# Opening of a two-layer encoder: where the squares are summed, where fillers stand, and where a quarter's rows are multiplied

## The chip, the cores and the metric

The kernel runs on one core of a Trainium2 chip. The metric is the device time of one execution, in microseconds (us), lower is better. The core's engines run side by side, each through its own list of instructions in a fixed order, and wait for each other through semaphores: TensorE (PE: matmuls; PEld is its loading of weights), VectorE (DVE), ScalarE (ACT), GpSimd (POOL) and SyncE (SP, which here issues the loads).

## What is computed

A trunk of two layers is applied to a sample of 512 tokens and a prompt of 256 tokens, each of width 1024, all in float32. Layer 0 mixes with an mLSTM in both directions, layer 1 with windowed attention; behind each comes a feed-forward network with a short convolution. Each of the four blocks begins with a normalization that is shifted and scaled by rows computed from a condition vector `c`:

```python
for l in range(DEPTH):
    mod = jax.nn.silu(c) @ adaln_w[l] + adaln_b[l]
    sh1, sc1, g1, sh2, sc2, g2 = [t[:, None, :] for t in jnp.split(mod, 6, axis=-1)]
    h = rmsnorm(x, norm_g[l, 0]) * (1 + sc1) + sh1
    proj = h @ w_in  # the mixer begins
    ...
    x = x + g1 * y
    h = rmsnorm(x, norm_g[l, 1]) * (1 + sc2) + sh2
    x = x + g2 * conv_ffn(h, ...)
return rmsnorm(x, final_g)
```

What matters here is the very first step of layer 0: `sh1` and `sc1` (2048 columns of `silu(c) @ adaln_w[0]`), the first normalization, and the first products `h @ w_in`.

## The kernel before

`x` lies transposed: 128 partitions, 8 chunks `c` of the width, 768 columns (columns 0 to 255 are the prompt, 256 to 767 the sample). The sample is normalized in two ranges of 256 columns, `r0` and `r1`; the prompt is `r2`. Products in float32 that must be precise are made of three: a high part and a low part of each operand (`hi`, `lo` for weights, `hh`/`hl`, with the tiles `zh`/`zl`, for the normalized input), and high x high, low x high, high x low are added in PSUM.

The method `opening` does everything up to the first four weight tiles' products (`i` = 0 is the gates' narrow weight, 1 and 2 the first query halves, 3 the first key half). In the part this is about, the order of PE, ACT, DVE and SP is the order in which the code is written (`manual_schedule`). Its steps:

- SP loads, in this order: the sample of `x` (4 loads), quarter 0's rows (4 loads), the narrow weight, the first weight's two halves, the rows of quarters 1 to 3 (12 loads; the last four go to `raw` buffers, of which there are five, and wait there for the narrow weight and the weight halves to be split), the prompt of `x`, and more.
- Statistics of the sample: `squares` (ACT, L919) squares each chunk into a buffer `nt`; `total` (PE, L927) multiplies the squares by a 128x2 tile of 1/1024 (`inv`), chunk by chunk into one PSUM group; `power` (DVE L935, POOL L936) adds EPS and raises to -1/2; `spread` (PE, `pa<-kct,nr`) spreads the result over the partitions into `pr`.
- Rows, for one quarter `i` of the 1024 columns (chunks 2i and 2i+1): `modulation(i, js)` (PE, L948) multiplies four blocks `j` of the loaded rows by the condition; `out` (DVE L957, ACT L958) copies the sums from PSUM; `turn` (PE, L962) turns them to the partitions; `factors` (DVE L969 to L971) makes shift and gain; `scaled` (DVE L974, ACT L975) makes `zh` of a chunk; `lower` (DVE L978) makes `zl`.
- `cast` and `rest` (ACT and DVE, L889 and L890) split a weight half.
- `sample(i, c)` is the three products of weight tile `i` and chunk `c` for the 512 sample columns (128x512, `ps<-zh,whi` and the like); `prompt(i, c)` is the same for the prompt.
- `warm(spare, n)` is `n` products of a tile of ones into a PSUM bank that is overwritten later: fillers.
- The prompt's statistics go through the class `Norm`: squares on ACT (L113), added on POOL (L122), and `next(factor)` brings first the total and the power (PE `pa<-inv,nt`, DVE L162, POOL L163) and then the spread.

In the profile, all products that go through the helper `mm` have the line L270. A 128x128 or 128x2 product in float32 leaves two records, a 32x256 product of `modulation` two as well.

Of the kernel before, what the change touches and what calls it, by code (L numbers as in the profile page):

```python
# [14 lines left out]
ALU = mybir.AluOpType  # L15

P = 128
D = 1024
KC = D // P
# [163 lines left out]
class Net:  # L183
# [660 lines left out]
    def opening(self, pool, sinks):  # L844

        nc, io = self.nc, self.io
# [3 lines left out]
        r0, r1, r2 = RANGES  # L850
# [49 lines left out]
        def sample(i, c, *za):  # L900
            for z, a in za or ((0, 0), (1, 0), (0, 1)):
                mm(z, i, a, c, S0, S1, 0, c == KC - 1 and (z, a) == (0, 1))
# [10 lines left out]
        turned = self.pa()  # L913
        half = {}

        def squares(rng, cs):
            for c in cs:
                sq = self.tmp([P, 256])
                act(sq, x(c)[:, rng[0] : rng[1]], AF.Square)  # L919
                half[rng, c] = sq  # L920

        def total(rng, cs):
            for c in cs:
                if c == 0:
                    half[rng] = self.pa()
                for b in range(2):
                    nc.tensor.matmul(  # L927
                        half[rng][:, 2 * b : 2 * b + 2], half[rng, c][:, b * P : (b + 1) * P], self.inv,
                        start=c == b == 0, stop=c == KC - 1, skip_group_check=True,
                    )  # L930

        def power(rng):
            r = half[rng, "r"] = self.nt.tile([P, 2], F32, tag="nr", name=self.nm("nr"), bufs=3)
            mean = half[rng][:, :4].rearrange("p (b s) -> p b s", s=2)[:, :, 0]
            nc.vector.tensor_scalar(r, mean, EPS, None, ALU.add)  # L935
            nc.gpsimd.tensor_tensor(r, r, self.mhalf[:, :2], ALU.pow)  # L936
# [6 lines left out]
        def modulation(i, js):  # L943
            for j in js:
                for z in range(2):
                    for g in range(2):
                        r = 32 * (2 * z + g)
                        nc.tensor.matmul(  # L948
                            sums[r : r + 32, :256], self.silc[:, 2 * j + z, :], rows[4 * i + j][:, z, 256 * g : 256 * g + 256],
                            start=j == 0, stop=j == 3, skip_group_check=True,  # L950
                        )
# [3 lines left out]
        def out(i):  # L955
            sides[i] = [self.tmp([P, P]) for _ in range(2)]
            nc.vector.tensor_copy(sides[i][0], sums[:, :P])  # L957
            nc.scalar.copy(sides[i][1], sums[:, P : 2 * P])  # L958
# [5 lines left out]
        def factors(i):  # L964
            c = 2 * i
            got = turned[:, 8 * i : 8 * i + 8].rearrange("p (b g s) -> p b g s", b=2, g=2)
            wide = lambda at: self.cst(at, 2).unsqueeze(2).to_broadcast([P, 2, 2])
            mod = self.mod[0]
            tt(mod[:, 8 + c : 10 + c], got[:, :, 1], wide(AB + 8 + c), ALU.add)  # L969
            stt(self.gain[0][0][:, c : c + 2], mod[:, 8 + c : 10 + c], 1.0, wide(NG + c), ALU.add, ALU.mult)  # L970
            tt(mod[:, c : c + 2], got[:, :, 0], wide(AB + c), ALU.add)  # L971

        def scaled(c):
            stt(x(c)[:, S0:S1], x(c)[:, S0:S1], gain(c, 0), pr, ALU.mult, ALU.mult)  # L974
            act(self.hh[:, c, S0:S1], x(c)[:, S0:S1], AF.Identity, bias=shift(c, 0))  # L975
# [18 lines left out]
        with self.tc.manual_schedule(engines={eng.PE, eng.Activation, eng.DVE}):  # L994
            for i in range(4):
                bank[i, 0] = self.ps()
            spare = bank[3, 0]
            squares(r0, range(KC))
            total(r0, range(KC))
            power(r0)  # L1000
            squares(r1, range(KC))
            modulation(0, (0,))
            spread(r0)
            total(r1, range(4))
            modulation(0, (1,))
            total(r1, range(4, KC))
            power(r1)
            modulation(0, (2,))
            spread(r1)
            self.warm(spare, 4)  # L1010
            modulation(0, (3,))
            out(0)
            self.warm(spare, 4)
            turn(0)
            narrow3 = narrow.rearrange("p (j m) -> p j m", m=4)
            hi0, lo0 = (t.rearrange("p (j m) -> p j m", m=32)[:, :, 0:4] for t in (hi[0], lo[0]))
            nc.scalar.copy(hi0, narrow3)
            tt(lo0, narrow3, hi0.bitcast(F32), ALU.subtract)
            factors(0)
            cast(1)  # L1020
            scaled(0)
            scaled(1)
            lower(0)
            rest(1)
            lower(1)
            cast(2)
            rest(2)
            self.warm(spare, 14)

            sample(0, 0)  # L1030
            sample(0, 1)
            modulation(1, (0,))
            for i in (1, 2):
                for c in (0, 1):
                    sample(i, c, *ph)
                if i == 1:
                    modulation(1, (1,))
            for i in (1, 2):
                for c in (0, 1):
                    sample(i, c, *pl)  # L1040
            modulation(1, (2,))
            self.warm(spare, 4)
            modulation(1, (3,))
            out(1)
            self.warm(spare, 4)
            turn(1)
            factors(1)
            for c in (2, 3):
                scaled(c)
            for c in (2, 3):  # L1050
                lower(c)
            modulation(2, (0,))
            self.warm(spare, 8)
            modulation(2, (1,))
            for i in range(3):
                sample(i, 2)
            modulation(2, (2,))
            sample(0, 3)
            modulation(2, (3,))
            out(2)  # L1060
            sample(1, 3)
            sample(2, 3)
            turn(2)
            factors(2)
            for c in (4, 5):
                scaled(c)
            for c in (4, 5):
                lower(c)
            modulation(3, (0,))
            modulation(3, (1,))  # L1070
            for i in range(3):
                sample(i, 4)
            modulation(3, (2,))
            sample(0, 5)
            modulation(3, (3,))
            out(3)
            sample(1, 5)
            sample(2, 5)
            turn(3)
            factors(3)  # L1080
            for c in range(4):
                norm.square(c)
            for c in (6, 7):
                scaled(c)
            for c in (6, 7):
                lower(c)
            for c in range(4, KC):
                norm.square(c)
            for z, (t0, t1) in enumerate(((0, 640), (640, 1024))):
                a, b = (kw[y][z].rearrange("p k m -> p (k m)") for y in range(2))  # L1090
                self.fp_copy_split(a, b, keys[:, t0:t1])
            self.warm(spare, 8)
            for c in (6, 7):
                for i in range(3):
                    sample(i, c)
            next(factor)
            for c in range(4):
                sample(3, c)
            next(factor, None)
            for c in range(4, KC):  # L1100
                sample(3, c)
            c0, c1, q = r2
            for i in range(3):
                bank[i, 1] = self.pa()

            def first(c):
                t = self.tmp([P, c1 - c0])
                stt(t, x(c)[:, c0:c1], gain(c, q), got[r2], ALU.mult, ALU.mult)
                act(self.hh[:, c, c0:c1], t, AF.Identity, bias=shift(c, q))
                return t  # L1110

            ts = {0: first(0)}
            for c in range(KC):
                if c + 1 < KC:
                    ts[c + 1] = first(c + 1)
                if c == 1:
                    sinks[0](0, bank[0, 0])
                if c in (3, 5):
                    sinks[c // 2](0, bank[c // 2, 0])
                stt(  # L1120
                    self.hl[:, c, c0:c1], ts.pop(c), shift(c, q), self.hh[:, c, c0:c1].bitcast(F32), ALU.add, ALU.subtract
                )
                for i in range(3):
                    prompt(i, c)
            bank[3, 1] = self.ps()
            for c in range(KC):
                prompt(3, c)
            self.opened = self.ahead(U_MIN + 1, 1)
            sinks[3](0, bank[3, 0])
# [828 lines left out]
```

## Time and profile before

| | |
|---|---|
| median of 3 runs | 1816.17 us (1815.19 to 1816.62) |
| the profiled execution | 1814.75 us, span 1813.0 us |
| mean granted TensorE clock | 0.998 |
| PE busy | 1779.3 us (98% of the span) |
| DVE busy | 1379.6 us (76%) |
| ACT busy | 895.3 us (49%) |
| POOL busy | 508.6 us (28%) |
| HBM | 176.77 MB read, 101 GB/s over the span |

All times inside the profile count from the span's start. A busy PE is not a PE at its peak, since matmuls are pipelined; the chain of waits tells more than the shares. In the first 45 us the loads are dense: the page's first slice moves 325 GB/s, against 102 GB/s on the average.

### The profile page before, as it was taken

The numbers are of one execution on the slowest core, as the hardware profiler recorded it, in microseconds if no ns is written. First come the engines' busy times: TensorE is split into PE (matmuls) and PEld (weight loads), VectorE is DVE, ScalarE is ACT, GpSimd is POOL, SyncE is SP. The second block draws the span as 40 slices with busy tenths as digits, with TensorE's granted clock in tenths as the row PEclk, the third lists the DMA queues.
The fourth block names the chain that finished last, engine by engine and source line by source line (L and its number), as shares of the span: only waits on it lengthen the run. The fifth ranks groups of instructions, "written<-read, shape, count | busy, mean of one in ns | idle before, by whom it ended". The sixth has DMA issues, their size and how long they took to land.

```text
span 1813.0 us, 28950 instructions
## 1 busy us (share of the span) xinstructions
PE 1779.3 (98%) x11220; PEld 1653.8 (91%) x11220; DVE 1379.6 (76%) x2183; ACT 895.3 (49%) x1810; POOL 508.6 (28%) x424
## 2 busy tenths in 40 slices
PE   8999999999999999999999999999999999999998
PEld 6798888989998999999999999889989999999998
DVE  2597777995799777777777867767998777777777
ACT  3445534454465444444444556665564444444443
POOL 0201210231024333333331313330144333333323
PEclk9999999999999999999999999999999999999999
DMA  8254556556212222222222321134122222222212
GB/s 325 71 176 157 199 190 213 186 179 206 81 57 78 63 70 70 66 64 69 70 70 83 117 88 47 54 96 131 56 82 70 70 70 70 70 70 70 70 36 70
DMA packets 64597, 185.09 MB, mean 102 GB/s; under 512 B 6231, under 2 KB 24311, under 8 KB 64332
## 3 DMA queue, kind: packets, MB, share of 16 engines
q1 hardware_dynamic: 63884, 182.72, 31.3%
q8 instruction: 88, 1.44, 0.3%
q10 hardware_dynamic: 576, 0.52, 0.1%
q14 instruction: 49, 0.40, 0.1%
HBM read 176.77 MB, written 6.44 MB: 101 GB/s over the span
## 4 chain that ended last, share of the span: by engine, by line
PE 83%; DVE 7%; DMA 4%; ACT 3%; issue 2%; POOL 1%; SPq 0%; POOLq 0%; DVEq 0%; ACTq 0%
PE ps L270 25%; PE pa L270 23%; PE ps L1447 10%; PE ps L1448 10%; PE ps L1450 10%; DMA raw<-in_adaln_t_dram 2%; DVE junk L480 2%; DMA raw<-in_w_dram 2%; PE pa L1286 1%; PE pa L927 1%; DVE wlo L277 1%; ACT whi L276 1%; PE pa L948 1%; PE pa L1447 0%; PE pa L1448 0%
## 5 line engine op out<-in xcount | busy, mean ns | idle before, releaser
L276 ACT CAST whi<-raw 128x1024 fp32r<-128x1024 f32 x229 | 239.7, 1048 | 341.1 <-PE pa L270 144.2
L277 DVE TENSOR_TENSOR wlo<-raw,whi 128x1024 fp32r<-128x1024 f32 x229 | 312.1, 1364 | 121.6 <-ACT whi L276 119.2
L270 PE MATMUL pa<-slab,whi 128*128 128x256 f32 (+1 forms) x1280 | 307.9, 336 | 0.0
L270 PEld LDWEIGHTS pa<-slab,whi 128*128 128x128 f32 x1280 | 222.1, 188 | 21.8 <-DVE slab L539 0.4
L539 DVE SCALAR_TENSOR_TENSOR slab<-pa,mod,slab 128x256 f32<-128x256 f32 (+1 forms) x320 | 187.2, 603 | 60.8 <-PE pa L270 60.7
L270 PE MATMUL pa<-slab,wlo 128*128 128x512 f32 (+1 forms) x640 | 205.5, 334 | 0.0
L270 PE MATMUL ps<-zh,whi 128*128 128x256 f32 (+1 forms) x520 | 178.9, 344 | 1.1 <-ACT zh L975 1.0
L1447 PE MATMUL ps<-zh,whi 128*128 128x384 f32 x504 | 172.4, 342 | 3.9 <-ACT nt L1518 2.0
L270 PE MATMUL ps<-zl,whi 128*128 128x256 f32 (+1 forms) x520 | 174.1, 336 | 0.8 <-DVE zl L505 0.5
L270 PE MATMUL ps<-slab,whi 128*128 128x384 f32 (+2 forms) x704 | 172.4, 330 | 2.2 <-ACT sg L838 1.3
L270 PE MATMUL ps<-zh,wlo 128*128 128x256 f32 (+1 forms) x520 | 173.0, 335 | 0.3 <-DVE wlo L277 0.3
L1448 PE MATMUL ps<-zl,whi 128*128 128x384 f32 x504 | 169.8, 337 | 0.8 <-DVE zl L1404 0.8
L1450 PE MATMUL ps<-zh,wlo 128*128 128x384 f32 x504 | 168.9, 335 | 0.0
L480 DVE CUSTOM_DVE_ANT_0 junk<-raw,crow,cstt 128x1024 f32<-128x1024 f32 x112 | 148.3, 1324 | 25.7 <-DMA raw<-in_adaln_t_dram 24.9
L1483 POOL TENSOR_TENSOR raw<-raw,raw 128x512 f32<-128x512 f32 x40 | 54.0, 1349 | 317.6 <-DVE wlo L277 245.5
L270 PEld LDWEIGHTS pa<-slab,wlo 128*128 128x128 f32 x640 | 120.5, 188 | 13.4 <-DVE wlo L277 0.4
L1699 POOL TENSOR_TENSOR slab<-slab 128x772 f32<-128x772 f32 x44 | 86.4, 1965 | 164.2 <-DVE slab L1687 152.2
L270 PEld LDWEIGHTS ps<-slab,whi 128*128 128x128 f32 x704 | 122.4, 188 | 4.9 <-ACT sg L838 1.5
L1686 DVE SCALAR_TENSOR_TENSOR slab<-slab,cstt,slab 128x771 f32<-128x771 f32 x88 | 103.8, 1181 | 26.6 <-ACT slab L1684 26.4
L270 PE MATMUL ps<-slab,wlo 128*128 128x384 f32 (+2 forms) x352 | 114.7, 327 | 0.1
L270 PEld LDWEIGHTS ps<-zh,whi 128*128 128x128 f32 x520 | 98.4, 189 | 17.3 <-issue 6.0
L1687 DVE SCALAR_TENSOR_TENSOR slab<-slab,cstt,slab 128x771 f32<-128x771 f32 x88 | 110.2, 1252 | 0.8
(316 smaller groups left out, 4320.9 us busy)
## 6 DMA issues: line engine op xcount, KB each, us to landing
raw<-in_w_dram SPq DMA_DIRECT2D x208, 512.0 KB, 3.8
raw<-in_adaln_t_dram SPq DMA_DIRECT2D x56, 512.0 KB, 4.5
raw<-in_adaln_w_dram SPq DMA_DIRECT2D x24, 512.0 KB, 4.6
slab<-in_x_dram SPq DMA_DIRECT2D x12, 512.0 KB, 6.0
slab<-in_adaln_h_dram SPq DMA_DIRECT2D x12, 512.0 KB, 9.2
slab<-mrows SPq DMA_DIRECT2D x8, 384.0 KB, 5.1
xs<-slab SPq DMA_DIRECT2D x6, 512.0 KB, 3.6
bt<-brow SPq DMA_DIRECT2D x16, 192.0 KB, 3.1
```

The source lines that it names most:

```text
L270: self.nc.tensor.matmul(out, lhsT, rhs, start=start, stop=stop)
L276: nc.scalar.copy(hi, src)
L277: return nc.vector.tensor_tensor(lo, src, hi.bitcast(F32), ALU.subtract)
L480: nc.vector.tensor_tensor_reduce(out=junk, in0=w, in1=row[:, s], scale=1.0, scalar=self.cst(AB + 48 * l + j), op0=ALU.mult, op1=ALU.add, a ...
L539: return self.nc.vector.scalar_tensor_tensor(x, o, self.mod[l][:, gc + c, q : q + 1], x, ALU.mult, ALU.add)
L1447: mm(o, wh[:, k], hi[k], start=start and k == 0, stop=False, skip_group_check=True)
L1448: mm(o, wh[:, k], lo[k], start=False, stop=False, skip_group_check=True)
L1450: mm(o, wl[:, k], hi[k], start=False, stop=k == 3, skip_group_check=True)
L1483: tt(q[0], q[2], q[0], ALU.subtract)
L1686: stt(y[:, 1:], u[:, :-1], w(0), y[:, 1:], ALU.mult, ALU.add)
L1687: stt(y[:, :-1], u[:, 1:], w(2), y[:, :-1], ALU.mult, ALU.add)
L1699: nc.gpsimd.tensor_tensor(y, y, yrow[:, j], ALU.mult)
```

## The change

Within `opening`, five things:

- The squares of a range are added up on DVE, seven adds of 128x256 for each range, into the first square's buffer, and `total` is one product for each half of the range instead of eight.
- Fillers: 30 ahead of range 0's total, 3, 2 and 2 between the next pieces, 3 and 10 (before: 4 and 14) ahead of the first products; those in quarters 1 to 3 shrink from 4, 4, 8 and 8 to one pair.
- `lower` of chunk 1 and `cast(2)` stand ahead of the first `rest`.
- The blocks, copies and turn of quarter i+1 stand among the products of quarter i (a helper `tiles` with a table of what follows which product), so that a turn comes two products (of three matmuls each) before the end of the quarter in front.
- The total of the prompt's squares comes after three of the eight last-tile products (before: ahead of all), the spread after six (before: after four).

The lists of ACT, POOL and SP are the same in both kernels, and behind the opening those of PE and DVE too. PE's list at its start, before (`inv` is the tile of 1/1024, `nt` are squares, `slab` with `silc` are rows and condition, `kct` with `nr` the spread):

```order
L927 MATMUL pa_193<-inv,nt_189 128x2 x2
L927 MATMUL pa_193<-inv,nt_191 128x2 x2
L948 MATMUL pa_169<-slab_111,silc 32x256 x4
L270 MATMUL pa_168<-kct,nr_210 128x128 x2
L927 MATMUL pa_235<-inv,nt_213 128x2 x2
L927 MATMUL pa_235<-inv,nt_215 128x2 x2
L927 MATMUL pa_235<-inv,nt_217 128x2 x2
L927 MATMUL pa_235<-inv,nt_219 128x2 x2
L948 MATMUL pa_169<-slab_111,silc 32x256 x4
```

and now, from PE's first instruction (`ones` are fillers):

```order
L270 MATMUL ps_176<-ones 128x128 x30
L270 MATMUL pa_230<-inv,nt_177 128x2 x2
L270 MATMUL ps_176<-ones 128x128 x3
L947 MATMUL pa_169<-slab_111,silc 32x256 x4
L270 MATMUL pa_168<-kct,nr_233 128x128 x2
L270 MATMUL ps_176<-ones 128x128 x2
L947 MATMUL pa_169<-slab_111,silc 32x256 x4
L270 MATMUL pa_274<-inv,nt_236 128x2 x2
L270 MATMUL ps_176<-ones 128x128 x2
L947 MATMUL pa_169<-slab_111,silc 32x256 x4
L270 MATMUL pa_168<-kct,nr_277 128x128 x2
L947 MATMUL pa_169<-slab_112,silc 32x256 x4
```

Of 32 two-column products four are left, and the fillers stand in front and between. DVE's list at the same place had nothing between its four memsets and the two adds of EPS; now:

```order
L921 TENSOR_TENSOR nt_177<-nt_177,nt_194 128x256
L921 TENSOR_TENSOR nt_177<-nt_177,nt_197 128x256
L934 TENSOR_SCALAR nr_233<-pa_230 128x2
L921 TENSOR_TENSOR nt_236<-nt_236,nt_238 128x256
L921 TENSOR_TENSOR nt_236<-nt_236,nt_241 128x256
```

The add of EPS of range 0 (L934), which reads range 0's total from PE, stands ahead of all adds of range 1. PE's list between quarter 1 and quarter 2, before (the L962 pair is turn 1, the products behind are chunk 2's):

```order
L270 MATMUL ps_175<-zh,wlo_161 128x512 x2
L948 MATMUL pa_169<-slab_113,silc 32x256 x4
L270 MATMUL ps_176<-ones 128x128 x4
L948 MATMUL pa_169<-slab_113,silc 32x256 x4
L270 MATMUL ps_176<-ones 128x128 x4
L962 MATMUL pa_170<-cstt,nt_350 128x4
L962 MATMUL pa_170<-cstt,nt_351 128x4
L948 MATMUL pa_169<-slab_113,silc 32x256 x4
L270 MATMUL ps_176<-ones 128x128 x8
L948 MATMUL pa_169<-slab_114,silc 32x256 x4
L270 MATMUL ps_173<-zh,whi_156 128x512
```

and now:

```order
L270 MATMUL ps_175<-zh,wlo_161 128x512 x2
L961 MATMUL pa_170<-cstt,nt_356 128x4
L961 MATMUL pa_170<-cstt,nt_357 128x4
L947 MATMUL pa_169<-slab_113,silc 32x256 x4
L270 MATMUL ps_176<-ones 128x128 x2
L947 MATMUL pa_169<-slab_114,silc 32x256 x4
L270 MATMUL ps_173<-zh,whi_156 128x512
L270 MATMUL ps_173<-zh,wlo_159 128x512
L270 MATMUL ps_173<-zl,whi_156 128x512
L947 MATMUL pa_169<-slab_114,silc 32x256 x4
```

Two of quarter 1's blocks have moved up in front of these rows, the turn follows the products at once, and quarter 2's third block stands behind the first three products of quarter 1.

```diff
-        def squares(rng, cs):
-            for c in cs:
+        def squares(rng):
+            for c in range(KC):
                 sq = self.tmp([P, 256])
                 act(sq, x(c)[:, rng[0] : rng[1]], AF.Square)
-                half[rng, c] = sq
...
+                if c:
+                    tt(half[rng], half[rng], sq, ALU.add)
+                else:
+                    half[rng] = sq
+
+        def total(rng):
+            pm = self.pa()
+            for b in range(2):
+                self.mm(pm[:, 2 * b : 2 * b + 2], half[rng][:, b * P : (b + 1) * P], self.inv, True, True)
+            half[rng] = pm
...
+            squares(r0)
+            self.warm(spare, 30)
+            total(r0)
             power(r0)
-            squares(r1, range(KC))
+            squares(r1)
+            self.warm(spare, 3)
             modulation(0, (0,))
             spread(r0)
-            total(r1, range(4))
+            self.warm(spare, 2)
             modulation(0, (1,))
-            total(r1, range(4, KC))
+            total(r1)
             power(r1)
+            self.warm(spare, 2)
             modulation(0, (2,))
             spread(r1)
-            self.warm(spare, 4)
             modulation(0, (3,))
...
+            def tiles(k, between):
+                for n, (c, i) in enumerate((c, i) for c in (2 * k, 2 * k + 1) for i in range(3)):
+                    sample(i, c)
+                    for f, *a in between.get(n, ()):
+                        f(*a)
+
+            operands(1)
+            tiles(1, {
+                0: [(modulation, 2, (2,))],
...
+            operands(2)
+            tiles(2, {0: [(modulation, 3, (2,))], 1: [(modulation, 3, (3,)), (out, 3)], 3: [(turn, 3)]})
             factors(3)
...
-            self.warm(spare, 8)
-            for c in (6, 7):
-                for i in range(3):
-                    sample(i, c)
-            next(factor)
-            for c in range(4):
+            tiles(3, {})
+            for c in range(KC):
                 sample(3, c)
-            next(factor, None)
-            for c in range(4, KC):
-                sample(3, c)
+                if c in (2, 5):
+                    next(factor, None)
```

More of the change, by code (lines that the diff above doesn't have):

```diff
@@ L914, in opening @@
         half = {}
-        def squares(rng, cs):
-            for c in cs:
+        def squares(rng):
+            for c in range(KC):
                 sq = self.tmp([P, 256])
                 act(sq, x(c)[:, rng[0] : rng[1]], AF.Square)
-                half[rng, c] = sq
[L922 to L930, printed above, removed]
+                if c:
[7 more added lines that the diff above has]
+            half[rng] = pm
         def power(rng):
@@ L997, in opening @@
             spare = bank[3, 0]
-            squares(r0, range(KC))
-            total(r0, range(KC))
+            squares(r0)
+            self.warm(spare, 30)
+            total(r0)
             power(r0)
-            squares(r1, range(KC))
+            squares(r1)
+            self.warm(spare, 3)
             modulation(0, (0,))
             spread(r0)
-            total(r1, range(4))
+            self.warm(spare, 2)
             modulation(0, (1,))
-            total(r1, range(4, KC))
+            total(r1)
             power(r1)
+            self.warm(spare, 2)
             modulation(0, (2,))
             spread(r1)
-            self.warm(spare, 4)
             modulation(0, (3,))
             out(0)
-            self.warm(spare, 4)
+            self.warm(spare, 3)
             turn(0)
@@ L1023, in opening @@
             lower(0)
-            rest(1)
             lower(1)
             cast(2)
+            rest(1)
             rest(2)
-            self.warm(spare, 14)
+            self.warm(spare, 10)
             sample(0, 0)
+            modulation(1, (0,))
             sample(0, 1)
-            modulation(1, (0,))
+            modulation(1, (1,))
             for i in (1, 2):
@@ L1035, in opening @@
                     sample(i, c, *ph)
-                if i == 1:
-                    modulation(1, (1,))
+                modulation(1, (i + 1,))
+            out(1)
             for i in (1, 2):
@@ L1040, in opening, with operands @@
                     sample(i, c, *pl)
[L1041 to L1045, printed above, removed]
-            turn(1)
[L1047 to L1051, printed above, removed]
+            turn(1)
             modulation(2, (0,))
-            self.warm(spare, 8)
+            self.warm(spare, 2)
             modulation(2, (1,))
-            for i in range(3):
[L1056 to L1079, printed above, removed]
+            def operands(i):
+                factors(i)
+                for c in (2 * i, 2 * i + 1):
+                    scaled(c)
+                for c in (2 * i, 2 * i + 1):
+                    lower(c)
+            def tiles(k, between):
[6 more added lines that the diff above has]
+                0: [(modulation, 2, (2,))],
+                1: [(modulation, 2, (3,)), (out, 2)],
+                3: [(turn, 2), (modulation, 3, (0,))],
+                5: [(modulation, 3, (1,))],
+            })
+            operands(2)
+            tiles(2, {0: [(modulation, 3, (2,))], 1: [(modulation, 3, (3,)), (out, 3)], 3: [(turn, 3)]})
             factors(3)
@@ L1091, in opening @@
                 self.fp_copy_split(a, b, keys[:, t0:t1])
-            self.warm(spare, 8)
-            for c in (6, 7):
-                for i in range(3):
-                    sample(i, c)
-            next(factor)
-            for c in range(4):
+            tiles(3, {})
+            for c in range(KC):
                 sample(3, c)
-            next(factor, None)
-            for c in range(4, KC):
-                sample(3, c)
+                if c in (2, 5):
+                    next(factor, None)
             c0, c1, q = r2
```

## The prediction

> **What bounds the kernel now.** In the page's chain of work that ended last TensorE (PE) stands first by far, so a saving must be a wait or work of PE that vanishes. I then read that chain in order of time over the first 120 us, since all edits lie in the first 85 us (columns: start, length, what), and the groups of the first 75 us (count, then busy us and mean ns of one):
>
> ```profile
> 6.32 0.42 ACT nt L919
> 6.79 6.99 PE pa L927 x32
> 13.77 1.01 PE pa L948 x8
> ...
> 24.77 1.22 PE pa L270 x4
> ```
>
> ```profile
> L927 PE MATMUL pa<-inv,nt 128*128 128x2 f32 x64 | 14.0, 351 | 6.8 <-ACT nt L919 6.8
> L270 PE MATMUL ps<-zh,wlo 128*128 128x512 f32 x24 | 8.9, 392 | 0.0
> ```
>
> The opening is bound by PE itself until 28.7: from 6.79 it is never idle, and the sums of squares (L927, 64 records of two columns) hold it for 14 us. All of it runs at half speed. The timeline (start, length, engine, line) shows that speed, and the marks against which I measure:
>
> ```profile
> 0.83 0.17 DVE L377 MEMSET ones<- 128x128 f32 x1 [0.83 <-PEq L1938]
> 6.32 2.61 ACT L919 ACTIVATE nt<-slab 128x256 f32<-128x256 f32 x8 [1.83 <-DMA slab<-in_x_dram]
> 25.79 1.91 PE L270 MATMUL ps<-ones 128*128 128x128 f32 x8
> 28.69 0.29 DVE L957 COPY nt<-pa 128x128 f32<-128x128 f32 x1 [4.75 <-PE pa L948]
> 29.83 3.37 PE L270 MATMUL ps<-ones 128*128 128x128 f32 x28
> 31.18 1.38 ACT L975 ACTIVATE zh<-slab,mod 128x512 fp32r<-128x512 f32 x2 [0.70 <-DVE slab L974]
> 32.96 0.48 PE L270 MATMUL ps<-zh,whi 128*128 128x512 f32 x1
> 62.95 0.50 PE L270 MATMUL ps<-zh,whi 128*128 128x512 f32 x1
> ```
>
> A filler is two records. Eight took 1.91 us at 25.8 (about 0.21 each from start to start), and 28 took 3.13 us between 29.83 and 32.96 (0.112 each). The full rate came about 3.7 us after dense products began at 24.77. The granted clock of the profile's rows reads full throughout and does not show it.
>
> Three marks, then: quarter 0's rows copied out at 28.69, first sample product S at 32.96, last quarter's first product T at 62.95.
>
> **Term A, start to the first copy-out.** The data limit this once PE does not. Landings, by windows that hold single issues (issue time, then time to landing):
>
> ```profile
> 9.91 1.81 ACT L919 ACTIVATE nt<-slab 128x256 f32<-128x256 f32 x5 [0.98 <-DMA slab<-in_x_dram]
> 4.89 0.43 SPq L406 DMA_DIRECT2D slab<-in_x_dram  x1
> DMA to landing us min/median/max: 6.3/6.3/6.3
> L862 SPq DMA_DIRECT2D slab<-in_adaln_h_dram x2: 430/576/722, 6.5 to 7.3; - x2
> DMA to landing us min/median/max: 8.5/8.8/9.1
> ```
>
> The second 256 columns of x land at 9.9 and 11.2, quarter 0's last rows at 7.3 + 9.1 = 16.4. SP's order and its waits up to there are unchanged, so these times stand.
>
> The added DVE work: 14 adds of 128x256. No such row exists in f32; the nearest are the 128x384 add and a 128x4 add, with the pow that follows:
>
> ```profile
> L122 DVE TENSOR_TENSOR nt<-nt,nt x26: 549/552/559, 440.4 to 1279.4; 128x384 f32<-128x384 f32 x26
> L969 DVE TENSOR_TENSOR mod<-pa,cstt 128x4 f32<-128x4 f32 x4 | 0.7, 163 | 4.4 <-PE pa L962 4.3
> 14.05 0.70 POOL L936 TENSOR_TENSOR nr<-nr,mhalf 128x2 f32<-128x2 f32 x1 [11.48 <-DVE nr L935]
> ```
>
> By size between 0.16 and 0.55 it is 0.42, with 0.04 for each add's wait on the one before: 0.46, so seven take 3.2 us. The first can start at about 7.1 (6.32, one square every 0.31, 0.42 long): range 0's sum stands at 10.3. The 30 fillers (60 records) start at 1.0: with the rate rising after 3.7 us, 17 records take 3.7 and 43 take 4.8, end 9.5; never rising, 60 x 0.213 = 12.8, end 13.8. I take 9.5 to 11, since the rise has no fixed time. So the fillers lie beside the load and the adds, and cost nothing unless the rate stays low.
>
> Range 0's total on PE (four records, 0.6 with its end) stands at 11.0. Behind it, on DVE, the small add of EPS (0.16) stands in front of range 1's seven adds: a new wait, behind which all range 1 is queued. These run 11.1 to 14.3; ScalarE's last square waits for the same total (it reuses that buffer) but is done by 12.6. Total 14.9, EPS add and pow to 15.9, spread (0.5) 16.4, then the modulation's last block. From that block's start to the copy is 0.71 (40.93 to 41.64 below): 17.1. With late fillers 17.8; I take **17.4, so A = 11.3** (at half speed throughout about 22, A = 6.6; at best the rows' landing sets 17.1, 11.6).
>
> **Term B, copy-out to S.** Before 4.27. The 28 filler records after the turn become 20: 0.9 off, and then zh (31.18 + 0.73, that is 3.2 after the copy) arrives at the same time. **B = 0.9** (0 to 1; at half speed -2).
>
> **Term C, S to T.** The rows of one quarter's end before, and the PE rates:
>
> ```profile
> 40.93 0.64 PE L948 MATMUL pa<-slab,silc 128*32 128x256 f32 x8
> 41.64 0.29 DVE L957 COPY nt<-pa 128x128 f32<-128x128 f32 x1 [6.02 <-PE pa L948]
> 42.50 0.51 PE L962 MATMUL pa<-cstt,nt 128*128 128x4 f32 x4
> 42.93 0.64 PE L948 MATMUL pa<-slab,silc 128*32 128x256 f32 x8
> 44.22 1.38 ACT L975 ACTIVATE zh<-slab,mod 128x512 fp32r<-128x512 f32 x2 [1.93 <-DVE slab L974]
> 47.78 0.39 PE L270 MATMUL ps<-zh,wlo 128*128 128x512 f32 x1
> 48.00 0.39 PE L270 MATMUL ps<-zl,whi 128*128 128x512 f32 x1
> 48.32 0.64 PE L948 MATMUL pa<-slab,silc 128*32 128x256 f32 x8
> 48.89 0.50 PE L270 MATMUL ps<-zh,whi 128*128 128x512 f32 x1
> 54.34 0.50 PE L270 MATMUL ps<-zh,whi 128*128 128x512 f32 x1 [0.99 <-ACT zh L975]
> ```
>
> A product costs 0.23. A modulation block adds 0.66 (48.00 to 48.89 is 0.89, less 0.23), a turn 0.43. From turn to the first zh is 2.4 us (42.50 to 44.22 + 0.7). Before: 54 x 0.23 + 12 x 0.66 + 3 x 0.43 + 48 filler records x 0.112 = 12.4 + 7.9 + 1.3 + 5.4 = 27.0 of the measured 29.99; the other 3.0 are waits at the quarters' ends, as at 54.34. After: 4 filler records instead of 48, so 22.1 of work. The turn now stands ahead of other quarters' products: turn 1 at S+7.0, zh at S+9.4 while PE has blocks until 9.2; turn 2 at 13.8, zh at 16.2, PE busy until 16.9; turn 3 at 21.0, zh at 23.4, PE busy until 22.8. Waits left: 0.2 at first, 0.2 and 0.3 at quarter 1, 0.6 at the last. T = S + 23.4, 6.6 less. My count leaves out semaphore steps that now show where fillers hid them; one more such wait of 0.3 to 0.4 at each of four quarter ends would leave 5. **C = 6.0**.
>
> Do the rows come in time? Quarter 3's last two are held back on SP's queue until DVE frees a raw buffer (SP's waits, and the last one's issue):
>
> ```profile
> SPq L862 <- DVE wlo L890: 3.6, 1, 3.6
> L862 SPq DMA_DIRECT2D raw<-in_adaln_h_dram x1: 328/328/328, 33.9 to 33.9; - x1
> ```
>
> That issue landed 4.2 us later. Both releasing instructions (the low parts of the weights) come 11 to 12 us earlier, so these rows land near 35 behind the queue, the prompt's x by 38; PE wants them at S + 19 = 39 and ScalarE wants x at 41. Three us of cover; without it PE waits for the difference.
>
> **Term D, T to the prompt.**
>
> ```profile
> 68.11 0.61 PE L270 MATMUL pa<-inv,nt 128*128 128x2 f32 x4 [0.44 <-POOL nt L122]
> 71.46 0.61 PE L270 MATMUL pa<-kct,nr 128*128 128x128 f32 x4
> 72.16 0.87 DVE L1108 SCALAR_TENSOR_TENSOR nt<-slab,gain,pa 128x256 f32<-128x256 f32 x2 [3.25 <-PE pa L270]
> ```
>
> The prompt's total moves from after 18 products to after 27, the spread from 12 to 9 products later. Before, spread = T + 8.5. After: 4.7 (18 products with a 0.5 wait) + 2.1 + 0.5 + 2.1 = T + 9.4. DVE and ScalarE pace the prompt from 72.16 on, so this is a loss: 0.8, or up to 1.35 if the total would have run earlier without its 0.44 wait. **D = -1.0.**
>
> **Sum.** 11.3 + 0.9 + 6.0 - 1.0 = 17.2 us. Behind the opening, the order of every engine is the same in both kernels, so all moves earlier together. The profiled execution took 1814.75 (span 1813.0), 1.4 below the median 1816.17; 1814.75 - 17.2 = 1797.6, by the median **1799.0**. What tells from no change is 0.2%, 3.6 us.
>
> [...]
>
> **Rivals.**
> *PE falls back to half speed between 11 and 17.* There PE works only in pieces (totals, blocks of 0.6, fillers of 0.2 to 0.7). For: 7 us of two-column records never raised the rate. Against: once up, the rate held through the 0.99 wait at 54.34 (the 24 wlo products average 392 ns). Price: spread and block 0.6 and 0.4 more (1.22 and 1.01 against 0.61 and 0.64), the total 0.3, turn and 20 filler records 2.4, then the rate rises as after 24.77: 3.5 to 6 off, gain 11 to 14, 1802 to 1805. [...]
> *The gain does not reach the end.* The mLSTM's stage waits for loads; were these to keep their times, the kernel would end near 1816.
>
> ```profile
> 114.65 8.62 DMA raw<-in_adaln_t_dram
> SPq L285 <- PE pa L948: 20.1, 3, 15.2
> ```
>
> Against: SP's loads behind the opening wait for buffers that the modulation blocks free (second row), and these come earlier too.
> *Slower: half speed through the whole opening.* If products broken up by blocks never raised the rate, A would be 6.6, B -2, and PE's 22 us from S to T would become 44: 6.6 - 2 + 6 - 22 - 1 = -12.4, near 1829. It decides when the half rate lasts more than 19 us past S (9.6 us of gain, lost at half a us per us). Against: between 33 and 63 blocks stand between products already, at full rate.
>
> **Chances.** Forecast 0.72 (1797 to 1802), half speed in the gap 0.18, no carry 0.06, slower 0.04. Faster 0.91, same 0.05, slower 0.04. The range for 8 in 10 runs from 1796.5 (C 6.6, D -0.8, A 11.6, and 1 us of spread between runs) to 1805, the dearer end of the first rival.
>
> **What would show it.** Filler records falling from 0.21 to 0.11 before 8 us; 14 adds of 0.42; copy-out near 17.4; S near 20.6; T near 44.6; spread 9.4 after T; the same distances after it. I am wrong if the block records between 11 and 20 run at half rate, if an add takes above 0.5, or if SP's quarter 3 rows land after 39.

## The result, and the profile after

The changed kernel takes 1797.01 us (median, 1796.71 to 1798.93), the kernel before 1815.82 beside it: a ratio of 0.9898, with a 95% interval of 0.9881 to 0.9916. A second comparison, on one chip with two experiments below, gave 1797.82 against 1815.10, 0.9901 (0.9887 to 0.9916). The gain is 17.3 to 18.8 us; 17.2 had been forecast. The profiled execution of the changed kernel took 1797.14 (span 1795.4).

The marks of the prediction, in us from the span's start:

| | before | forecast | after | term | gained (forecast) |
|---|---|---|---|---|---|
| first copy-out | 28.69 | 17.4 | 18.07 | A | 10.62 (11.3) |
| S, first sample product | 32.96 | 20.6 | 21.30 | B | 1.04 (0.9) |
| T, last quarter's first product | 62.95 | 44.6 | 46.16 | C | 5.13 (6.0) |
| spread of the prompt | 71.46 | T + 9.4 | 55.38 | D | -0.71 (-1.0) |

Together 16.1, which is also the distance between the two traces a little further on (ScalarE's third table load: 90.37 before, 74.28 after). No mark shows the other 1 to 3 us; they come behind the opening, and whether they belong to the change is taken up below.

The groups of TensorE (PE) in the first 75 us of the changed kernel (count, busy us, mean ns of one, idle us just before them and what ended it):

```profile
L270 PE MATMUL ps<-ones 128*128 128x128 f32 x104 | 16.1, 318 | 1.0 <-DVE ones L377 1.0
L947 PE MATMUL pa<-slab,silc 128*32 128x256 f32 x96 | 7.7, 391 | 1.0 <-ACT nt L919 1.0
L270 PE MATMUL pa<-zl,whi 128*128 128x256 f32 x24 | 7.1, 295 | 2.2 <-DVE zl L1105 2.2
```

The group that held PE for 14 us, the two-column products of L927, is gone. The first wait left is one of 1.0 for squares, the largest one of 2.2 in the prompt, where PE waits for DVE.

The timeline from the start to the first sample product, several engines (start, length, engine, line, tiles, count; in brackets the idle time ahead and its releaser):

```profile
1.05 9.71 PE L270 MATMUL ps<-ones 128*128 128x128 f32 x60 [1.05 <-DVE ones L377]
6.84 3.61 DVE L921 TENSOR_TENSOR nt<-nt,nt 128x256 f32<-128x256 f32 x7 [5.54 <-ACT nt L919]
10.60 0.51 PE L270 MATMUL pa<-inv,nt 128*128 128x2 f32 x4
11.22 3.59 DVE L921 TENSOR_TENSOR nt<-nt,nt 128x256 f32<-128x256 f32 x7
15.06 0.61 PE L270 MATMUL pa<-inv,nt 128*128 128x2 f32 x4
15.94 0.70 POOL L935 TENSOR_TENSOR nr<-nr,mhalf 128x2 f32<-128x2 f32 x1 [3.75 <-DVE nr L934]
16.72 0.71 PE L270 MATMUL pa<-kct,nr 128*128 128x128 f32 x4
17.36 0.64 PE L947 MATMUL pa<-slab,silc 128*32 128x256 f32 x8
18.07 0.29 DVE L956 COPY nt<-pa 128x128 f32<-128x128 f32 x1 [2.20 <-PE pa L947]
20.42 1.38 ACT L974 ACTIVATE zh<-slab,mod 128x512 fp32r<-128x512 f32 x2 [0.57 <-DVE slab L973]
21.30 0.48 PE L270 MATMUL ps<-zh,whi 128*128 128x512 f32 x1
```

The way to the copy-out is now the chain of adds on VectorE (DVE), the total, the power, the spread and a modulation block. A block of eight records takes 0.64, as it does at the full rate (1.08 at half, in E1 below). Of the front fillers, the records stand 0.213 apart up to 6.76 and 0.112 from there on; they reach up to the first total and end with it.

At the other end of the opening:

```profile
46.16 0.50 PE L270 MATMUL ps<-zh,whi 128*128 128x512 f32 x1 [0.48 <-ACT zh L974]
52.83 0.50 PE L270 MATMUL pa<-inv,nt 128*128 128x2 f32 x4
55.38 0.61 PE L270 MATMUL pa<-kct,nr 128*128 128x128 f32 x4
56.08 0.87 DVE L1093 SCALAR_TENSOR_TENSOR nt<-slab,gain,pa 128x256 f32<-128x256 f32 x2 [2.55 <-PE pa L270]
```

The prompt's total stands 6.7 behind T, its spread 9.2, and DVE takes it up 0.7 later, as before.

### The profile page after: what moved, and what is told of

Same layout as the page of the kernel before. It is cut to its first block, busy times and chain, and to the rows that moved or that the text cites. A ratio compares the mean times of both kernels' runs of the same rounds, so it can differ in the third digit from the quotient of the medians.

```text
span 1795.4 us, 28879 instructions
## 1 busy us (share of the span) xinstructions
PE 1767.6 (98%) x11176; PEld 1643.5 (92%) x11176; DVE 1390.7 (77%) x2197; ACT 895.4 (50%) x1810; POOL 509.1 (28%) x424
## 4 chain that ended last, share of the span: by engine, by line
PE 85%; DVE 6%; DMA 3%; ACT 3%; issue 2%; POOL 1%; SPq 0%; POOLq 0%; DVEq 0%; ACTq 0%
PE ps L270 27%; PE pa L270 23%; PE ps L1432 10%; PE ps L1433 10%; PE ps L1435 10%; DMA raw<-in_adaln_t_dram 2%; DVE junk L480 2%; PE pa L1271 1%; DVE wlo L277 1%; DMA raw<-in_w_dram 1%; PE pa L1432 0%; PE pa L1433 0%; PE pa L947 0%; DVE s1l L277 0%; ACT whi L276 0%
```

## Experiments

The theory: the adds and the front fillers gain A + B together, since two-column products neither raise PE's rate nor keep it; the new order of the quarters gains C; the later total of the prompt loses D. Rivals: the fillers do nothing that the adds don't do alone, or the adds nothing that an early rate wouldn't; the rate falls back in the stretch from 11 to 18 us; the part of the gain that no mark shows comes from elsewhere.

### E1: the changed kernel without the front fillers

```diff
             squares(r0)
-            self.warm(spare, 30)
             total(r0)
```

> The changed kernel without the 30 fillers ahead of range 0's total; all else as changed. Theory 'the fillers buy the full rate': without them PE works at 0.21 us a record until dense work has lasted some 4 to 7 us, so range 0's total ends about 0.4 later than 11.1, spread, blocks and turn cost nearly double up to about 22, copy-out comes near 19.1 (now 18.07), the 20 filler records behind the turn at half rate, S at 23.5 to 25 (now 21.3). Time 2.5 to 4.5 us more than the changed kernel: 1799.5 to 1801.5. Rival 'the chain of adds and landings covers PE anyway': S within 1 us of 21.3, time within 1 us of the changed kernel's 1797.0.

Measured: 1800.28 us, ratio 0.9917 (0.9901 to 0.9934). PE's timeline, total, spread and a block:

```profile
10.64 1.01 PE L270 MATMUL pa<-inv,nt 128*128 128x2 f32 x4 [10.64 <-DVE nt L921]
14.08 1.23 PE L270 MATMUL pa<-kct,nr 128*128 128x128 f32 x4
19.11 1.08 PE L947 MATMUL pa<-slab,silc 128*32 128x256 f32 x8
25.23 0.48 PE L270 MATMUL ps<-zh,whi 128*128 128x512 f32 x1
```

The total begins at the same time as with fillers (10.64 against 10.60), so 60 records of filler cost nothing there; but blocks take 1.08 instead of 0.64 and the spread 1.23 instead of 0.71, up to 21. S comes 3.9 later, and so does everything behind it (table load 78.23 against 74.28). The copy-out stands at 22.00, not near 19.1 as expected, and S a little past the range. With the adds in place the front fillers are worth 3.9 us by the trace, 2.5 to 3.3 by the medians.

From the total on, PE's list here is that of the changed kernel, and PE is busy by the profile without a break until the rate rises at 21.35. So the same pieces that kept the rate in the changed kernel did not raise it here for 10.7 us (10.64 to 21.35; the expected 4 to 7 were an estimate, beside the 3.7 seen in the kernel before and the 5.7 in the changed one's first trace), and only eight of their records are two-column ones. What kept the rate down in the kernel before need not be the two-column products alone, though for its first 7 us PE had nothing else.

### E2: the kernel before with the front fillers alone

```diff
             squares(r0, range(KC))
+            self.warm(spare, 30)
             total(r0, range(KC))
```

> The kernel before with only the 30 fillers put ahead of its first total; sums stay on PE in 32 two-column products. Theory 'the rate, once up, is kept by two-column products': fillers end at 10.6, the 64 records take 0.111 instead of 0.213, copy-out near 23.2 instead of 28.69, gain 5.5 us, 1810.3. [...]

Measured: 1816.15 us (1813.39 to 1819.98 in ten runs), ratio 1.0005 (0.9995 to 1.0014). The fillers reached the 0.112 spacing at 6.12, and then the two-column products began (PE's timeline, then windows with the busy time and count of PE, PEld, DVE, ACT and POOL, the granted clock, the DMA share and GB/s):

```profile
10.26 4.37 PE L927 MATMUL pa<-inv,nt 128*128 128x2 f32 x32
...
10.00:12.90 2.90, 2.90 (x29) 2.90 (x28) 0.00 (x0) 1.93 (x5) 0.00 (x0) 1.00 1.02 418
12.90:20.00 7.10, 7.07 (x37) 6.18 (x37) 0.16 (x1) 1.40 (x4) 0.70 (x1) 0.50 1.03 409
20.00:29.90 9.90, 9.88 (x55) 7.13 (x55) 0.34 (x2) 0.00 (x0) 0.70 (x1) 0.50 1.03 410
30.00:40.00 10.00, 9.81 (x73) 7.47 (x72) 5.75 (x11) 3.73 (x6) 0.00 (x0) 1.00 0.55 166
```

PE is busy by the profile for all of the 2.90 us up to 12.90, nearly all of them two-column products, and then the granted clock is 0.50: the rate was not kept but lost after 2.7 us of these products (10.26 to 12.95), and it does not come back until 30. The copy-out stands at 29.71, not near 23.2 as expected and one us later than before (the fillers hold the first products back to 10.26). An early rate alone is worth nothing here. E1 and E2 together, at S, which lies ahead of the new quarters: the adds without the front fillers bring 7.7 (32.96 - 25.23), the front fillers alone -1.3 (S at 34.22), both 11.7. The 7.7 and the 11.7 hold the small fillers and term B too, since E1 and the changed kernel have them.

### E3: the statistics and their fillers alone; E4: the quarters alone

E3 is the kernel before with the adds, the one-product totals and the fillers 30, 3, 2, 2, 3 of the changed one, and the quarters as they were. E4 is the changed kernel with the squares summed on PE and no fillers among the statistics but the old 4 and 4.

```diff
 E3, against the kernel before:
-            squares(r0, range(KC))
-            total(r0, range(KC))
+            squares(r0)
+            self.warm(spare, 30)
+            total(r0)
...
 E4, against the changed kernel:
-            squares(r0)
-            self.warm(spare, 30)
-            total(r0)
+            squares(r0, range(KC))
+            total(r0, range(KC))
```

> The kernel before with the squares added on VectorE and the fillers up to quarter 0's turn as changed; quarters, their fillers, the order of the weights' low parts and the prompt's total as before. Terms A and B add to the rest: copy-out at 18.07 as in the changed kernel, S near 22.2 (28 filler records behind the turn instead of 20), and from S on the spans of before: T = S + 30 = 52.2. Shift behind the opening 10.6 to 10.8, gain 10.6 us, or up to 12.3 if the 1.6 us that the mLSTM stage gained in the changed kernel come with any earlier start: 1803.5 to 1805.2. Rival 'the rows' landing or the held buffers eat it': T later than 53.

> The changed kernel with the statistics of before: sums on PE in two-column products, no fillers in front; the quarters' blocks and turns, the order of the low parts, 10 fillers behind turn 0 and the prompt's total as changed. S near 32.0 (0.9 earlier than 32.96), T = S + 24.9 = 56.9 (before 62.95), then 0.7 lost at the prompt: shift behind the opening 5.4, gain 5.4 us, up to 7 with the mLSTM stage's 1.6: 1808.8 to 1810.4. Together with the third of these runs it should add up to the whole. Rival 'the two halves overlap': here more than 7.5, because the earlier quarters then hide part of what the statistics cost.

Measured: E3 1803.48 us, ratio 0.9939 (0.9924 to 0.9954); E4 1808.90, ratio 0.9967 (0.9954 to 0.9980), against 1815.61 beside them. Gains 12.1 and 6.7, sum 18.8. The first lines are E3's (copy-out, S), the last two E4's (S and T, from PE's timelines):

```profile
17.95 0.29 DVE L956 COPY nt<-pa 128x128 f32<-128x128 f32 x1 [2.20 <-PE pa L947]
22.07 0.48 PE L270 MATMUL ps<-zh,whi 128*128 128x512 f32 x1
```

```profile
32.76 0.48 PE L270 MATMUL ps<-zh,whi 128*128 128x512 f32 x1
57.65 0.50 PE L270 MATMUL ps<-zh,whi 128*128 128x512 f32 x1 [0.48 <-ACT zh L975]
```

T - S is 30.06 in E3, as before, and 24.89 in E4, as in the changed kernel. The two parts are nearly independent: by the marks 10.8 and 5.3 at T, and 16.8 for the whole. The 0.7 left over is in front of S, where E3 still has the 28 filler records that the whole has cut to 20 (term B): its S is 0.8 later than the changed kernel's. E4 has the 20, but its S was expected near 32.0 and is only 0.2 ahead of the kernel before: its rate rose at 29.9 only, and the 8 filler records ahead of the turn took 1.80 instead of 1.16.

### E5 and E7: the prompt's total earlier again

E7 undoes term D: the two steps of the prompt's statistics come behind the last tile's products 0 and 2. E5 does this too, and in quarter 0 puts the last modulation block ahead of the spread of range 1.

```diff
             modulation(0, (2,))
-            spread(r1)
             modulation(0, (3,))
+            spread(r1)
...
-                if c in (2, 5):
+                if c in (0, 2):
                     next(factor, None)
```

> The changed kernel, with the prompt's modulation row multiplied ahead of the first quarters' spread and one tile of the factor put behind the last quarter's tiles 0 and 2 instead of 2 and 5, so that the total for the prompt can stand some 2 us earlier. In the changed kernel the spread's products begin at T + 9.2 (55.38 - 46.16). Theory 1 (the prompt's start waits for its total, and the copy-out for fillers in front): copy-out at 17.4 instead of 18.07, spread at T + 7.0, all behind it 2.0 to 2.8 us earlier: 1794.2 to 1795.1. Theory 2 (products or ScalarE's work on the tiles bound the way to the prompt): spread at T + 8.5 or later, gain under 1 us: 1796.2 to 1797.5.

Measured: 1794.94 us (1794.26 to 1795.66), ratio 0.9885 (0.9868 to 0.9901). The spread stands at 53.09, 7.1 behind T (45.98), as expected. The expectation speaks of the prompt's row; the block that was moved is the last one of quarter 0's rows, which the sample needs.

> The changed kernel with one edit: the two tiles of the factor stand behind the last quarter's tiles 0 and 2 instead of 2 and 5, so that the prompt's total stands earlier among the products. Theory 1 (the place of the total alone makes term D): copy-out and S as in the changed kernel (18.07, 21.3), spread at T + 7.1 instead of 9.2, about 2.1 us under the changed kernel. Theory 2 (the spread waits for something else, and the earlier modulation row made the gain): spread at T + 8.5 or later, under 1 us gained.

> The earlier prompt row and the earlier total once more, beside the changed kernel: if the 2.3 us by which its prompt moved is what the time shows, about 2.3 below the changed kernel of this call; if part of the 1794.94 was scatter behind the opening, within 1 us of it.

> The changed kernel once more, beside the two below on one chip: about 1797 (1796.7 to 1798.9 so far).

Measured beside each other: E7 1795.41 (1794.34 to 1796.70), E5 1794.76 (1794.42 to 1796.59), the changed kernel 1797.82 (1796.41 to 1798.00). The ratios to before are 0.9889 (0.9873 to 0.9906), 0.9888 (0.9874 to 0.9903) and 0.9901 (0.9887 to 0.9916); the intervals overlap, so the times alone don't settle 2 us; the marks show them within the opening. E7, from PE's timeline, then E5's copy-out and S:

```profile
46.07 0.50 PE L270 MATMUL ps<-zh,whi 128*128 128x512 f32 x1 [0.50 <-ACT zh L974]
51.33 0.50 PE L270 MATMUL pa<-inv,nt 128*128 128x2 f32 x4
53.17 0.61 PE L270 MATMUL pa<-kct,nr 128*128 128x128 f32 x4
```

```profile
17.41 0.29 DVE L956 COPY nt<-pa 128x128 f32<-128x128 f32 x1 [1.42 <-PE pa L947]
21.09 0.48 PE L270 MATMUL ps<-zh,whi 128*128 128x512 f32 x1
```

In E7 the spread comes at T + 7.1 and the table load at 72.08, 2.2 earlier than in the changed kernel: the place of the total was the whole of term D, and PE had room for it (it is even 1.4 better than before, T + 8.5). The earlier block moves E5's copy-out by 0.66, but S by 0.21 only, since the spread it displaced now stands between the copies and the turn. So the better version is E7's edit; the other one adds 0.1 to 0.3 at the table load (71.98 and 71.82 in E5's two traces), no more than three traces of the changed kernel differ among themselves (74.01 to 74.28).

### E6: without the small fillers between the pieces

```diff
             squares(r1)
-            self.warm(spare, 3)
             modulation(0, (0,))
...
-            self.warm(spare, 2)
...
-            self.warm(spare, 2)
...
-            self.warm(spare, 3)
             turn(0)
```

> The changed kernel without the ten small fillers that stand between its statistics pieces and silc products (3, 2, 2 and 3); the 30 in front and the 10 behind the copy-out stay. Theory 1 (products of two columns count as idle and the small fillers hold the rate): the rate falls to half within the stretch 11 to 18 us, copy-out 1 to 1.5 us later, S some 3 us later than 21.30: 1799 to 1801. Theory 2 (the 128x256 silc products and the 30 fillers suffice): the rate stays, S within 1 us of 21.30, perhaps 0.5 earlier: 1796 to 1798.

Measured: 1802.26 us (1799.17 to 1803.27), ratio 0.9923 (0.9909 to 0.9938). PE's timeline and the windows behind it:

```profile
12.98 0.64 PE L947 MATMUL pa<-slab,silc 128*32 128x256 f32 x8
14.96 0.61 PE L270 MATMUL pa<-inv,nt 128*128 128x2 f32 x4 [1.34 <-DVE nt L921]
15.49 0.64 PE L947 MATMUL pa<-slab,silc 128*32 128x256 f32 x8
16.59 1.08 PE L270 MATMUL pa<-kct,nr 128*128 128x128 f32 x4 [0.46 <-POOL nr L935]
...
14.00:16.60 2.60, 1.18 (x13) 0.69 (x13) 0.96 (x3) 0.00 (x0) 0.70 (x1) 1.00 1.04 410
16.60:20.00 3.40, 2.99 (x17) 1.88 (x17) 0.58 (x2) 0.86 (x3) 0.00 (x0) 0.53 1.03 407
20.00:23.50 3.50, 3.50 (x17) 3.50 (x18) 3.18 (x8) 2.71 (x4) 0.00 (x0) 0.50 1.03 410
```

The rate falls at about 16.7, after a stretch in which PE works 1.18 of 2.60 us, and stays at half for 7 us: copy-out at 18.76 instead of 18.07, S at 23.93 instead of 21.30, table load at 76.67 instead of 74.28. So the rival of the fall in the gap is a real mechanism of this kernel, and in this trace nothing but the ten small fillers was missing. The fall does not seem to come each time: of the four executions, three have a mean granted clock of 0.995 to 0.996 and took 1801.48 to 1803.27, and the fourth has 0.998 and took 1799.17; the changed kernel's eight timed executions have 0.998 or 0.999. The marks give 2.4 us; the median is 4.4 to 5.3 over the changed kernel, above the 1799 to 1801 expected, and the rest of that lies behind the opening, where traces scatter (next).

### The kernel before and the changed kernel once more

> The kernel before once more, for a second trace. From the third ACT table load to the last one it took 267.98 us in its first trace, the changed kernel 266.18. Theory 1 (the new quarter part or what it moves changes something there): 267.7 to 268.6 again. Theory 2 (it varies from one execution to the next): anywhere from 266 to 269.

> The changed kernel once more, for a second trace. From the third ACT table load to the last one it took 266.18 us in its first trace. Theory 1 (the difference belongs to the kernel): 265.9 to 266.5 again. Theory 2 (it varies from one execution to the next): anywhere from 266 to 269.

Each of these is one execution (1813.41 and 1798.85 us). ScalarE's third table load and its last one of the mLSTM stage, from these second traces of the kernel before and of the changed kernel:

```profile
89.92 1.28 ACT L632 ACT_TABLE_LOAD   x1
357.16 1.28 ACT L838 ACT_TABLE_LOAD   x1
```

```profile
74.19 1.28 ACT L632 ACT_TABLE_LOAD   x1
342.46 1.28 ACT L838 ACT_TABLE_LOAD   x1
```

Between these two loads every engine has the same list in all kernels of this study. The stretch took 267.98 and 267.24 in the kernel before, and 266.18, 268.27 and 267.23 in three traces of the changed one; the other kernels with the old quarters gave 268.25 (E2) and 268.59 (E3), those with the new ones 265.99 (E1), 266.37 (E4), 266.47 and 266.28 (E5), 266.17 (E7) and 269.00 (E6). So one kernel varies by 2 us there from one execution to the next, and the 1.8 between the first two traces says nothing. The means, 268.0 of four and 266.9 of nine, leave room for about 1 us by the new quarters; whether there is one stays open. The start varies less: the table load stood at 90.37 and 89.92, and at 74.28, 74.19 and 74.01, a gain of 16.0 in the opening. The copy-out stood at 28.69 and 28.20, and at 18.07, 17.97 and 17.80, so that each term is good to about half a us.

## Why the prediction was right, step by step

**The mechanism** held in all four terms: E1 and E2 show the two halves of A, E3 and E4 part A and B from C, and E7 shows D. The forecast of 1799.0 is 2.0 above the first measurement and 1.2 above the second. The terms came to 16.1 instead of 17.2; the measured gain of 17.3 to 18.8 is 1 to 3 us more than these terms, and no term had that. So what the terms missed was made up by something outside the prediction, whose size alone differs by 1.5 us between the two comparisons: that part of the agreement is luck. Two small sums of the prediction do not come out: by its own terms S is 20.8 and T 44.8 (17.4 + 4.27 - 0.9, and 24.0 more) instead of 20.6 and 44.6, and the lower end of its range is 1796.9 (1816.17 - 18.3 - 1) instead of 1796.5.

**A, 10.6 instead of 11.3.** The add of 128x256 itself takes 0.42, as estimated from its neighbours:

```profile
L921 DVE TENSOR_TENSOR nt<-nt,nt x14: 416/425/426, 6.8 to 14.4; 128x256 f32<-128x256 f32 x14
```

The mis-sized term is what one add waits for the one before: the adds stand 0.53 apart from start to start, 0.11 of it the wait, where the prediction allowed 0.04, which no run shows, and seven take 3.6 us instead of 3.2. In range 0 this hardly shows, since its first add began at 6.84 instead of 7.1 and the first total at 10.60 was as early as said. Range 1's adds, queued behind the small add of EPS as forecast (11.22), ended at 14.81 instead of 14.3, and the total began at 15.06: PE had the block of 14.49 in front of it, another 0.2. From there the lengths are those of the forecast but for the spread, behind which the last block began 0.7 after the power's end instead of 0.5. The 17.4 had 0.3 in it for late fillers, so 0.7 of these 1.0 is left as the miss. The front fillers ended with the first total, within the 9.5 to 11 given, though the rate rose after 5.7 us instead of 3.7 (after 3.7 in the second trace).

**B** as forecast: with 20 filler records instead of 28, `zh` arrives (20.42 + 0.73) as the last of them end. The way from the copy-out to S took 3.23, against 4.13 in E3, which has the 28.

**C, 5.1 instead of 6.0.** The counted 27.0 of work before left 3.0, all taken for waits at the quarters' ends, of which 1.3 were to stay: 1.7 of the forecast. By the profile PE had less idle time than that to lose (from S to T, the kernel before and then the changed one):

```profile
32.96:62.95 29.99, 28.67 (x213) 18.55 (x212) 11.69 (x26) 6.11 (x14) 2.19 (x3) 1.00 0.55 187
21.30:46.16 24.86, 24.12 (x169) 13.23 (x167) 12.58 (x27) 7.00 (x15) 2.22 (x3) 1.00 1.02 396
```

PE, the first busy time in each line, is idle for 1.32 us before and 0.74 after: 0.6 of wait went, not 1.7. The rest of the 3.0 was work that the count had left out. One part of it can be read from the rows, since a block between two products costs more than the 0.66 taken (changed kernel):

```profile
22.41 0.64 PE L947 MATMUL pa<-slab,silc 128*32 128x256 f32 x8
22.98 0.50 PE L270 MATMUL ps<-zh,whi 128*128 128x512 f32 x1
23.31 0.39 PE L270 MATMUL ps<-zh,wlo 128*128 128x512 f32 x1
23.55 0.40 PE L270 MATMUL ps<-zl,whi 128*128 128x512 f32 x1
```

The product behind a block holds PE for 0.33, the next for 0.24. The prediction measured a block up to the product behind it and left out this 0.1, which stands behind eleven of the twelve blocks before (behind three of them a filler record holds PE for 0.21 instead of 0.11) and behind all twelve after: 1.1 of the 3.0. As much is added behind a turn (44.03 to 44.36) and behind the wait at 46.16 (to 46.50), so what causes it is open. Before, then, 28.1 of work, 1.3 of idle time and 0.6 not accounted for; after, 22.1 + 1.2 = 23.3, 0.7 and 0.8. The lower end of the range given, 5, came from a guess at semaphore steps of about this size; the cause was another. The rows of quarter 3 were in time, as said: the last was issued at 25.1 and landed 10.2 later, at 35.3, with the queue's wait for a raw buffer gone.

```profile
L862 SPq DMA_DIRECT2D raw<-in_adaln_h_dram x4: 328/328/328, 21.2 to 25.1; - x4
...
DMA to landing us min/median/max: 10.2/10.2/10.2
```

**D, -0.7 instead of -1.0,** within its 0.8 to 1.35 but for 0.1; E7 shows that it was a choice of place and not a cost of the rest.

**The rivals.** Half speed in the gap did not happen in three traces of the changed kernel, and E6 shows that the small fillers stood against it. The reason given against it was weak: the rate survived the wait of 0.99 at 54.34 among dense products, and did not survive E6's wait of 1.34 among sparse ones (which of the two, the length or the neighbours, decides was not tried). Its price, 3.5 to 6 off, was too high for the opening (2.4), though E6's median is 4.4 to 5.3 off. The gain did reach the end, and half speed through the whole opening happened nowhere: in E1, E2 and E4 it ended at 21, 30 and 30, ahead of S each time.

**The rise and the fall of the rate.** The prediction took the rise to have no fixed time, beside the one rise that the kernel before shows. The runs bear this out: from fillers beginning at 1.05 the rise came between 4.5 (E3) and 7.1 (E5) in nine traces of six kernels, 3.5 to 6.1 us on, and in three traces of the changed kernel at 6.8, 4.8 and 6.6. E6's second rise, at 23.6, came 3.6 after its fillers began at 19.98. The fall in E6 came behind a stretch in which PE was busy for 1.18 of 2.60 us, the one in E2 with PE busy for 2.90 of 2.90: idle time by the profile is not what the two have in common, and what brings a fall is not shown. The 60 filler records of E3 show the early rise, against 9.71 us for the same 60 in the first trace of the changed kernel:

```profile
1.05 8.59 PE L270 MATMUL ps<-ones 128*128 128x128 f32 x60 [1.05 <-DVE ones L377]
```

## What to carry to other kernels

Before a reduction is put on TensorE because it has time to spare, ask what rate it will run at: 7 us of nothing but two-column records did not raise PE's rate in the kernel before, and where it had been raised, in E2, it was lost after 2.7 us of them. Two remedies that go together (the sums elsewhere, and fillers in front and between) must be judged together: here the adds without the front fillers brought 7.7 us at S, the front fillers alone lost 1.3, and both brought 11.7. And when work is counted against a measured stretch, the difference is not all wait: the idle time of the engine in that stretch bounds what can be gained from waits (here 1.3 of a supposed 3.0).

## What the runs showed that had not been expected

- TensorE lost its rate in E2 while it was busy without a gap by the profile (2.90 of 2.90 us up to 12.90, granted clock 0.50 behind it), with records that were nearly all two-column products.
- The granted clock of the profile's rows shows a fall once there has been a rise (0.50 in E2 and E6), but not the low rate at the start. E1's records stand at half rate from 10.6 to 21, and a window over them reads 1.00:

```profile
11.00:22.00 11.00, 11.00 (x63) 7.26 (x63) 3.20 (x9) 1.10 (x4) 1.51 (x2) 1.00 1.03 412
```

- The rate changed three times within one trace: in E2 it rose at 6.1, fell at 13.0 and rose again at 30.0, in E6 at 6.5, 16.8 and 23.6. So it stayed at half for about 17 us in E2 and about 7 in E6, though PE was busy by the profile for 16.95 of 17.00 us there (12.90 to 29.90) and for 6.49 of 6.90 here (16.60 to 23.50). What sets the length of such a stretch is not shown.
